# A two-block network on one core: the head norms of attention branch C computed chunk by chunk instead of in one table at the end

## The chip, the cores and the metric

The kernel runs on one core of a Trainium2 chip. The core has five engines that run side by side, each through its own list of instructions in a fixed order: TensorE (PE in the profile; its weight loads are listed apart, as PEld), VectorE (DVE), ScalarE (ACT), GpSimd (POOL), and SyncE (SP), from which all data transfers are started. The metric is the device time of one execution in microseconds (us). Three runs of the kernel before took 1641.73, 1644.12 and 1644.69 us; the median is 1644.12 us.

## The reference

The reference passes 256 tokens of width 1024 through a first block (a mixer of convolution, pooling and attention, then a mixture of experts) and then through two layers of a second block. A layer of the second block is a feed-forward network, a mixer with three attention branches, and another feed-forward network; 16 learned tokens stand in front, so that 272 tokens are processed. The change touches branch C of the mixer, where queries (eight heads of 64) and keys (two heads of 64) are normalised per head before the rotation:

```python
def rms_norm_2(x, g):
    xf = x.astype(jnp.float32)
    y = xf * lax.rsqrt(jnp.mean(xf * xf, axis=-1, keepdims=True) + EPS)
    return (y * g.astype(jnp.float32)).astype(x.dtype)
...
    n = rms_norm_2(h, mix_norm[l])          # the mixer's input
    qa, ka, va, qb, kb, vb, qc, kc, vc, gates = jnp.split(n @ w_in, offsets, axis=-1)
...
    qc = apply_axial_rope(rms_norm_2(heads(qc, C_Q_HEADS), qn), row, col)
    kc = apply_axial_rope(rms_norm_2(heads(kc, C_KV_HEADS), kn), row, col)
    oc = dense_block_attention(qc, kc, heads(vc, C_KV_HEADS))
```

Since every channel of a head is divided by the same number, the division of a query head can be done on its scores later, and that of a key head on the rotated key.

## The kernel before

Everything is stored transposed: 128 channels by 272 tokens in a tile. A linear layer takes its weights from one long stream of units of eight 128x128 tiles, which SP loads into `raw` buffers (line 362). Each chunk of four weight tiles is split in two: ScalarE rounds it to `h` (line 378), and VectorE computes the rest `l = raw - h` (line 395). TensorE then runs three matmuls for each weight tile (lines 509 to 511, `mm3`): `h` with the low part of the input, `h` with its high part, and `l` with its high part. `h` has 9 buffers and `l` 7, and splitting runs some six chunks ahead of the matmuls. So VectorE has to deliver one `l` for each twelve matmuls.

The mixer's input projection (`Mixer.fillers`, section `z0` or `z1` of the stream) has one output tile after the other. For branch C these are, in this order, the key tile `kc`, four query tiles `qc` 0 to 3 (two heads each) and the value tile `vc`. `linear` yields twice in each output tile of eight weight tiles, after four of them each; such a yield is a tick. `Weave.run` counts the ticks: at each it first runs what `after(n, f)` put off until then, and then events of the attention (scores, softmax, transposes), so that the small work of attention stands between the matmuls of the projection. The source order made in this way is then arranged, when the program is built, into one fixed list for each engine: an instruction may be moved past others that it doesn't depend on. On the chip each engine runs its list strictly in order, and waits where an operand isn't ready.

What is done to a `qc` or `kc` tile (`Mixer.evac`): ScalarE copies it out of PSUM and squares it into a tile `t` (line 1553; two such buffers). Two ticks later `head_squares` sums the squares of each head with tiny matmuls into a PSUM tile `ph` (line 1657, three matmuls for 272 tokens), and VectorE copies the sums into a table `ssq` of 3x10 columns (line 1659). After the last one, `qc` 3, `norm_c` turns the whole table into factors: `rsqrt` computes mean plus epsilon on VectorE (`rsa`, line 558), then raises it to the power -0.5 on GpSimd (`rsy`, line 559). Line 1668 multiplies the eight query columns by 1/8 on VectorE; the result `qscale` later scales the scores. Three ticks on, `keys` spreads the key columns over the channels with matmuls into `pb` (line 620, `spread`), multiplies the rotated key by them (line 1672) and cuts the key into parts `kk` and `kl` (lines 1605 to 1607, the last a transfer on SP). In the first layer, `meta` computes `mscale` for the 16 extra tokens five ticks on.

Besides, the value tile `vc` is scaled into `t` on VectorE (line 1544), transposed on TensorE into `pv` (line 1627), and its last 16 tokens are laid out by six GpSimd instructions in `vd` (lines 1642 to 1644), which TensorE transposes into `pw` (line 1632). The first block ends with the convolution's last activation on ScalarE (`cv`, line 1059), a small product `pc`, and its result `mix` (line 1069), which the last output product needs.

Of the kernel before, what the change touches and what calls it, by code (L numbers as in the profile page):

```python
# [7 lines left out]
F32 = mybir.dt.float32  # L8
# [4 lines left out]
ALU = mybir.AluOpType  # L13
# [5 lines left out]
S = 256  # L19
META = 16  # L20
T = S + META
EPS = 1e-6
# [5 lines left out]
HD = 64  # L28
# [421 lines left out]
class Kernel:  # L450
# [97 lines left out]
        o, _ = PARAMS[name]  # L548
        return self.par[:, o + j:o + j + n]

    def rsqrt(self, src, shape, mul, add=EPS):

        v = self.nc.vector
        a, y = (self.tiny.tile(shape, F32, name="rs" + n, bufs=2) for n in "ay")
        if isinstance(add, float):
            v.tensor_scalar(a, src, mul, add, op0=ALU.mult, op1=ALU.add)
        else:
            v.scalar_tensor_tensor(a, src, mul, add, op0=ALU.mult, op1=ALU.add)
        self.nc.gpsimd.tensor_tensor(y, a, self.halves[:, :1].to_broadcast(shape), op=ALU.pow)  # L559
        self.radicand = a  # L560
        return y
# [145 lines left out]
class Block1:  # L707
# [243 lines left out]
    def head_squares(self, kind, i, s):  # L951
        K, nc = self.K, self.nc
        c = 2 * (i % 2) + (kind == "k")
        if c == 0:
            self.ssq = self.p2.tile([128, 2, 8], F32, name="ssq1")
        q = K.ps.tile([128, 512], F32, name="ph", tag="t", bufs=2)
        for j in range(2):
            nc.tensor.matmul(q[:, 2 * j:2 * j + 2], s[:, 128 * j:128 * j + 128], K.table("half"), start=True, stop=True)
        nc.vector.tensor_copy(self.ssq[:, :, 2 * c:2 * c + 2], q[:, :4].rearrange("p (j r) -> p j r", r=2))
        if c == 3:  # L960
            self.norm_qk(i - 1)
# [533 lines left out]
class Mixer:  # L1495
# [7 lines left out]
    def run(self, after):  # L1503
        K, nc, l, n = self.K, self.nc, self.l, self.n
        self.gates = K.big.tile([128, 24, T], F32, name="gates", tag="bigA")
        self.ob = K.big.tile([128, 24, T], F32R, name="ob", tag="bigB")
        self.oh, self.ol = self.ob[:, :12], self.ob[:, 12:]
        self.rb = K.norm_rows(T)
        self.ssq = None
        self.after = K.after  # L1510
        first = 18 if n == T else 16
        K.weave.run(self.fillers(), self.events(), first, 2 * len(Z_MS) + 18)
        self.finish(after)


    def fillers(self):
# [7 lines left out]
    def evac(self, m, p):  # L1524
        K, nc = self.K, self.nc
        kind, i = Z_MS[m]
# [20 lines left out]
        if kind in ("qb", "kb"):  # L1547
            self.parts(kind, i, z)
        elif kind in ("vb", "va", "vc"):
            self.values(kind, i, z)  # L1550
        elif kind in ("qc", "kc"):
            s = K.tmp.tile([128, T], F32, name="t2")[:, :w]
            nc.scalar.activation(s, p, AF.Square)
            self.after(2, lambda: self.head_squares(kind, i, s))

    def swap(self, kind, i, z):

# [86 lines left out]
        nc.gpsimd.tensor_copy(d[:, b], d[:, a])  # L1644

    def head_squares(self, kind, i, s):
        K, nc = self.K, self.nc
        w = s.shape[1]
        if self.ssq is None:
            self.ssq = K.tiny.tile([128, 3, 10], F32, name="ssq")  # L1650
            if self.n == S:
                nc.gpsimd.memset(self.ssq, 0.0)
        c = 4 if kind == "kc" else i
        p = K.ps.tile([128, 512], F32, name="ph", tag="t", bufs=2)
        cuts = [0, 128] if w == S else [0, 128, T - 128]
        for j, o in enumerate(cuts):
            nc.tensor.matmul(p[:, 2 * j:2 * j + 2], s[:, o:o + 128], K.table("half"), start=True, stop=True)  # L1657
        nj = len(cuts)
        nc.vector.tensor_copy(self.ssq[:, :nj, 2 * c:2 * c + 2], p[:, :2 * nj].rearrange("p (j r) -> p j r", r=2))
        if (kind, i) == ("qc", 3):  # L1660
            self.norm_c()

    def norm_c(self):

        K, nc = self.K, self.nc
        y = K.head_rsqrt(self.ssq, [128, 3, 10])
        self.qscale = K.tiny.tile([128, 3, 8], F32, name="qscale", bufs=1)
        nc.vector.tensor_scalar(self.qscale, y[:, :, :8], HD ** -0.5, None, op0=ALU.mult)

        def keys():  # L1670
            z = self.turned_c.pop(("kc", 0))
            nc.vector.tensor_mul(z, z, K.spread(y[:, :, 8:10], T))
            self.parts("kc", 0, z)

        def meta():

            d = K.tmp.tile([128, 8, META], F32, name="vq", bufs=1)
            nc.gpsimd.tensor_tensor(d, K.table("ident")[:, 128 - META:].unsqueeze(1).to_broadcast([128, 8, META]),
                                    self.qscale[:, 2].unsqueeze(2).to_broadcast([128, 8, META]), op=ALU.mult)
            p = K.ps.tile([128, 512], F32, name="pq", tag="t", bufs=2)  # L1680
            nc.tensor.matmul(p[:, :1], d.rearrange("p c m -> p (c m)"), K.table("ones")[:, :1], start=True, stop=True)
            self.mscale = K.tiny.tile([128, 1], F32, name="mscale", bufs=1)
            nc.vector.tensor_copy(self.mscale, p[:, :1])

        self.after(3, keys)
        if self.n == T:
            self.after(5, meta)


    def events(self):  # L1690
# [265 lines left out]
```

## Time and profile before

| | |
|---|---|
| median of three runs | 1644.12 us (1641.73 to 1644.69) |
| the profiled execution | 1641.68 us |
| its span, first to last instruction | 1639.8 us |
| TensorE busy | 1590.8 us, 97% |
| VectorE busy | 1153.9 us, 70% |
| ScalarE busy | 955.9 us, 58% |
| GpSimd busy | 255.9 us, 16% |
| mean granted TensorE clock | 0.987 of full speed |

The profile shows one execution. A row of the timeline gives the start, the duration, the engine, the line, the operation and its tiles; in brackets stands how long the engine had been idle before it, and which instruction ended that. The table of windows gives busy times in a stretch and the granted clock of TensorE, as a share of full speed. [...] The two mixers of the second block, in which the change lies, run their projections from about 515 us (first layer) and 1190 us (second layer).

### The profile page before, as it was taken

What the parts mean: (1) busy time and instruction counts of PE and PEld (TensorE: products, weight loads), DVE (VectorE), ACT (ScalarE), POOL (GpSimd) and SP (SyncE); (2) the same over time, 40 slices, a digit from 0 to 9 for tenths busy, and PEclk for the clock granted to TensorE, in tenths of its full rate; (3) what the DMA queues carried; (4) which work ended last, traced back from release to release, by engine and by line L of the source; (5) the groups of instructions that cost most, each with busy time, mean ns of one, the idle gap of its engine ahead of it and who ended that gap; (6) DMA issues with size and microseconds to landing.
All of it is one profiled execution on the core that took longest, in us unless ns stands there. A gap on an engine that the chain in (4) does not pass through costs nothing.

```text
span 1639.8 us, 32660 instructions
## 1 busy us (share of the span) xinstructions
PE 1590.8 (97%) x12034; PEld 1517.1 (93%) x12034; DVE 1153.9 (70%) x2433; ACT 955.9 (58%) x2002; POOL 255.9 (16%) x493
## 2 busy tenths in 40 slices
PE   7989999899999989999999999999998999999997
PEld 6877777799999979999999999999998999999997
DVE  6757888867666867668777666766677776877753
ACT  7526777655554757665655555555566776565552
POOL 2111000200001444342000010000034333200000
PEclk9999999999999999999999999999999999999998
DMA  7336889355554534454555555555553454455552
GB/s 265 104 134 226 333 309 322 131 179 173 175 175 159 168 113 134 148 166 155 182 171 177 171 177 168 177 171 179 169 170 127 139 166 158 161 193 189 183 189 82
DMA packets 87253, 289.80 MB, mean 177 GB/s; under 512 B 11696, under 2 KB 17328, under 8 KB 86960
## 3 DMA queue, kind: packets, MB, share of 16 engines
q1 hardware_dynamic: 87088, 287.66, 52.3%
q8 instruction: 96, 1.57, 0.4%
q14 instruction: 69, 0.57, 0.1%
HBM read 282.18 MB, written 1.05 MB: 173 GB/s over the span
## 4 chain that ended last, share of the span: by engine, by line
PE 74%; DVE 3%; POOL 2%; issue 1%; ACT 1%; DMA 0%; SPq 0%; DVEq 0%; POOLq 0%; ACTq 0%
PE acc L509 23%; PE acc L511 23%; PE acc L510 23%; PE po L1873 1%; PE pt L1849 1%; DVE l L395 1%; PE sc L1812 1%; PE sc L1813 1%; POOL rsy L559 1%; PE pb L620 0%; DVE ob L1597 0%; DVE xl L579 0%; PE pt L1859 0%; PE ph L1657 0%; DMA zs<-gates 0%
## 5 line engine op out<-in xcount | busy, mean ns | idle before, releaser
L378 ACT ACTIVATE h<-raw 128x512 fp32r<-128x512 f32 x996 | 621.7, 631 | 509.8 <-PE acc L510 400.3
L395 DVE TENSOR_TENSOR l<-raw,h 128x512 fp32r<-128x512 f32 x996 | 692.2, 701 | 232.1 <-PE acc L511 197.8
L509 PE MATMUL acc<-xl,h 128*128 128x272 f32 (+1 forms) x2288 | 669.7, 293 | 6.9 <-ACT h L378 6.8
L511 PE MATMUL acc<-xh,l 128*128 128x272 f32 (+1 forms) x2288 | 659.0, 288 | 0.8 <-DVE l L395 0.8
L510 PE MATMUL acc<-xh,h 128*128 128x272 f32 (+1 forms) x2288 | 656.9, 287 | 0.0
L509 PEld LDWEIGHTS acc<-xl,h 128*128 128x128 f32 x2288 | 434.6, 190 | 16.0 <-issue 8.2
L511 PEld LDWEIGHTS acc<-xh,l 128*128 128x128 f32 x2288 | 434.2, 190 | 1.1 <-DVE l L395 1.0
L510 PEld LDWEIGHTS acc<-xh,h 128*128 128x128 f32 x2288 | 434.5, 190 | 0.2
L511 PE MATMUL acc<-ah,l 128*128 128x272 f32 (+1 forms) x704 | 202.2, 287 | 0.0
L509 PE MATMUL acc<-al,h 128*128 128x272 f32 (+1 forms) x704 | 202.2, 287 | 0.0
L510 PE MATMUL acc<-ah,h 128*128 128x272 f32 (+1 forms) x704 | 201.5, 286 | 0.0
L595 POOL TENSOR_TENSOR sqacc<-sqacc,sq 128x272 f32<-128x272 f32 (+1 forms) x53 | 45.4, 857 | 797.5 <-ACT sq L591 796.6
L511 PEld LDWEIGHTS acc<-ah,l 128*128 128x128 f32 x704 | 132.7, 188 | 0.0
L509 PEld LDWEIGHTS acc<-al,h 128*128 128x128 f32 x704 | 132.6, 188 | 0.0
L510 PEld LDWEIGHTS acc<-ah,h 128*128 128x128 f32 x704 | 132.6, 188 | 0.0
L509 PE MATMUL acc<-ob,h 128*128 128x272 f32 (+1 forms) x320 | 92.5, 290 | 0.0
L510 PE MATMUL acc<-ob,h 128*128 128x272 f32 (+1 forms) x320 | 90.9, 284 | 0.0
L511 PE MATMUL acc<-ob,l 128*128 128x272 f32 (+1 forms) x320 | 90.8, 285 | 0.0
L664 DVE TENSOR_TENSOR t<-acc,rb 128x272 f32<-128x272 f32 (+1 forms) x88 | 38.5, 437 | 63.5 <-PE acc L511 63.5
L1777 POOL TENSOR_SCALAR P<-P,r 128x272 f32<-128x272 f32 x48 | 54.8, 1142 | 122.8 <-DVE r L1775 101.1
L509 PEld LDWEIGHTS acc<-ob,h 128*128 128x128 f32 x320 | 60.2, 188 | 2.0 <-issue 1.2
L510 PEld LDWEIGHTS acc<-ob,h 128*128 128x128 f32 x320 | 60.3, 188 | 0.0
(353 smaller groups left out, 1999.5 us busy)
## 6 DMA issues: line engine op xcount, KB each, us to landing
raw<-in_stream_dram SPq DMA_DIRECT2D x523, 512.0 KB, 3.3
bias<-in_rpb_dram SPq DMA_DIRECT2D x16, 272.0 KB, 3.2
zs<-gates SPq DMA_DIRECT2D x48, 34.0 KB, 2.2
kk<-kk SPq DMA_DIRECT2D x24, 68.0 KB, 2.0
X<-in_x_dram SPq DMA_DIRECT2D x4, 256.0 KB, 5.5
tab<-in_tables_dram SPq DMA_DIRECT2D x1, 1024.0 KB, 7.2
zs<-gates SPq DMA_DIRECT2D x32, 32.0 KB, 2.2
out_dram<-out SPq DMA_DIRECT2D x4, 256.0 KB, 2.2
```

The costliest lines, as they stand in the source:

```text
L378: self.nc.scalar.activation(h, src, AF.Copy)
L395: self.nc.vector.tensor_sub(l, src, h.bitcast(F32))
L509: mm(out, h, xl, start=start, stop=False)
L510: mm(out, h, xh, start=False, stop=False)
L511: mm(out, l, xh, start=False, stop=stop)
L559: self.nc.gpsimd.tensor_tensor(y, a, self.halves[:, :1].to_broadcast(shape), op=ALU.pow)
L595: (nc.vector if k == KC - 1 else nc.gpsimd).tensor_add(self.sqs[0], self.sqs[0], s)
L664: nc.vector.tensor_mul(u, p, rb)
L1777: (nc.gpsimd if h else nc.vector).tensor_scalar(P[:, h, keys], P[:, h, keys], r[:, h:h + 1], None, op0=ALU.mult)
L1812: nc.tensor.matmul(sc[h][:, :T], q[:, h, s], k[:, h], start=True, stop=False)
L1813: nc.tensor.matmul(sc[h][:, :T], q[:, h, s], kl[:, h], start=False, stop=True)
L1849: nc.tensor.transpose(p[:, 128 * (2 * c + h):128 * (2 * c + h) + 128], P[:, h, 128 * c:128 * c + 128], ident)
```

## The change

`norm_c` and the table `ssq` are gone. `head_squares` now runs four ticks after the tile instead of two, and finishes its own columns: VectorE adds the epsilon straight from PSUM, and GpSimd raises six columns (four for the queries of the second layer) to the power. For queries the result goes straight into `qscale`: the factor 1/8 is folded in by working with the sum instead of the mean and with 64 times epsilon (`scaled_eps`, a small GpSimd instruction, one for each layer). For the key, `norm_keys` runs four ticks after its squares, instead of three after `qc` 3. `meta_scale` runs four ticks after `qc` 3's squares.

```diff
--- before.py
+++ after.py
@@ -548,10 +548,12 @@
         o, _ = PARAMS[name]
         return self.par[:, o + j:o + j + n]
 
-    def rsqrt(self, src, shape, mul, add=EPS):
+    def rsqrt(self, src, shape, mul, add=EPS, y=None):
 
         v = self.nc.vector
-        a, y = (self.tiny.tile(shape, F32, name="rs" + n, bufs=2) for n in "ay")
+        a = self.tiny.tile(shape, F32, name="rsa", bufs=2)
+        if y is None:
+            y = self.tiny.tile(shape, F32, name="rsy", bufs=2)
         if isinstance(add, float):
             v.tensor_scalar(a, src, mul, add, op0=ALU.mult, op1=ALU.add)
         else:
@@ -1506,11 +1508,16 @@
         self.ob = K.big.tile([128, 24, T], F32R, name="ob", tag="bigB")
         self.oh, self.ol = self.ob[:, :12], self.ob[:, 12:]
         self.rb = K.norm_rows(T)
-        self.ssq = None
         self.after = K.after
+        self.after(3, self.scaled_eps)
         first = 18 if n == T else 16
         K.weave.run(self.fillers(), self.events(), first, 2 * len(Z_MS) + 18)
         self.finish(after)
+
+    def scaled_eps(self):
+
+        self.eps_head = self.K.tiny.tile([128, 3], F32, name="epsh", bufs=1)
+        self.nc.gpsimd.tensor_scalar(self.eps_head, self.K.eps_tok, float(HD), None, op0=ALU.mult)
 
 
     def fillers(self):
@@ -1551,7 +1558,7 @@
         elif kind in ("qc", "kc"):
             s = K.tmp.tile([128, T], F32, name="t2")[:, :w]
             nc.scalar.activation(s, p, AF.Square)
-            self.after(2, lambda: self.head_squares(kind, i, s))
+            self.after(4, lambda: self.head_squares(kind, i, s))
 
     def swap(self, kind, i, z):
 
@@ -1644,47 +1651,42 @@
         nc.gpsimd.tensor_copy(d[:, b], d[:, a])
 
     def head_squares(self, kind, i, s):
+
         K, nc = self.K, self.nc
         w = s.shape[1]
-        if self.ssq is None:
-            self.ssq = K.tiny.tile([128, 3, 10], F32, name="ssq")
-            if self.n == S:
-                nc.gpsimd.memset(self.ssq, 0.0)
-        c = 4 if kind == "kc" else i
         p = K.ps.tile([128, 512], F32, name="ph", tag="t", bufs=2)
         cuts = [0, 128] if w == S else [0, 128, T - 128]
+        nj = len(cuts)
         for j, o in enumerate(cuts):
             nc.tensor.matmul(p[:, 2 * j:2 * j + 2], s[:, o:o + 128], K.table("half"), start=True, stop=True)
-        nj = len(cuts)
-        nc.vector.tensor_copy(self.ssq[:, :nj, 2 * c:2 * c + 2], p[:, :2 * nj].rearrange("p (j r) -> p j r", r=2))
-        if (kind, i) == ("qc", 3):
-            self.norm_c()
-
-    def norm_c(self):
-
-        K, nc = self.K, self.nc
-        y = K.head_rsqrt(self.ssq, [128, 3, 10])
-        self.qscale = K.tiny.tile([128, 3, 8], F32, name="qscale", bufs=1)
-        nc.vector.tensor_scalar(self.qscale, y[:, :, :8], HD ** -0.5, None, op0=ALU.mult)
-
-        def keys():
-            z = self.turned_c.pop(("kc", 0))
-            nc.vector.tensor_mul(z, z, K.spread(y[:, :, 8:10], T))
-            self.parts("kc", 0, z)
-
-        def meta():
-
-            d = K.tmp.tile([128, 8, META], F32, name="vq", bufs=1)
-            nc.gpsimd.tensor_tensor(d, K.table("ident")[:, 128 - META:].unsqueeze(1).to_broadcast([128, 8, META]),
-                                    self.qscale[:, 2].unsqueeze(2).to_broadcast([128, 8, META]), op=ALU.mult)
-            p = K.ps.tile([128, 512], F32, name="pq", tag="t", bufs=2)
-            nc.tensor.matmul(p[:, :1], d.rearrange("p c m -> p (c m)"), K.table("ones")[:, :1], start=True, stop=True)
-            self.mscale = K.tiny.tile([128, 1], F32, name="mscale", bufs=1)
-            nc.vector.tensor_copy(self.mscale, p[:, :1])
-
-        self.after(3, keys)
-        if self.n == T:
-            self.after(5, meta)
+        ssq = p[:, :2 * nj].rearrange("p (j r) -> p j r", r=2)
+        shape = [128, nj, 2]
+        if kind == "kc":
+            y = K.rsqrt(ssq, shape, 1.0 / HD, K.eps_tok.unsqueeze(2).to_broadcast(shape))
+            self.after(4, lambda: self.norm_keys(y))
+            return
+        if i == 0:
+            self.qscale = K.tiny.tile([128, 3, 8], F32, name="qscale", bufs=1)
+        K.rsqrt(ssq, shape, 1.0, self.eps_head[:, :nj].unsqueeze(2).to_broadcast(shape), self.qscale[:, :nj, 2 * i:2 * i + 2])
+        if i == 3 and self.n == T:
+            self.after(4, self.meta_scale)
+
+    def norm_keys(self, y):
+        K, nc = self.K, self.nc
+        z = self.turned_c.pop(("kc", 0))
+        nc.vector.tensor_mul(z, z, K.spread(y, T))
+        self.parts("kc", 0, z)
+
+    def meta_scale(self):
+
+        K, nc = self.K, self.nc
+        d = K.tmp.tile([128, 8, META], F32, name="vq", bufs=1)
+        nc.gpsimd.tensor_tensor(d, K.table("ident")[:, 128 - META:].unsqueeze(1).to_broadcast([128, 8, META]),
+                                self.qscale[:, 2].unsqueeze(2).to_broadcast([128, 8, META]), op=ALU.mult)
+        p = K.ps.tile([128, 512], F32, name="pq", tag="t", bufs=2)
+        nc.tensor.matmul(p[:, :1], d.rearrange("p c m -> p (c m)"), K.table("ones")[:, :1], start=True, stop=True)
+        self.mscale = K.tiny.tile([128, 1], F32, name="mscale", bufs=1)
+        nc.vector.tensor_copy(self.mscale, p[:, :1])
 
 
     def events(self):
```

How the change moves instructions: three places. The first is VectorE in the first layer, where branch C's last norms fall (`rsa`, `ssq` and `qscale` as above; `t` is the scaled value tile or a gate, `ob` the low parts of queries). Before:

```order
L1659 COPY ssq<-ph 128x3x2
L1842 TENSOR_REDUCE mpm<-pt 96x64
L558 SCALAR_TENSOR_TENSOR rsa<-ssq,eps_7975 128x30
L395 TENSOR_TENSOR l<-raw,h 128x512
L1597 TENSOR_TENSOR ob<-gates,ob 64x272 x2
L1668 TENSOR_SCALAR qscale<-rsy 128x24
L1544 TENSOR_TENSOR t_8861<-acc,rb 128x272
L395 TENSOR_TENSOR l<-raw,h 128x512
L1576 SCALAR_TENSOR_TENSOR gates<-gates,par,tab 128x272
L1577 SCALAR_TENSOR_TENSOR zs<-zs,par,tab 128x272
```

and now, from the reduction `mpm` on:

```order
L1844 TENSOR_REDUCE mpm<-pt 96x64
L395 TENSOR_TENSOR l<-raw,h 128x512
L1604 TENSOR_TENSOR ob<-gates,ob 64x272 x2
L1551 TENSOR_TENSOR t_8879<-acc,rb 128x272
L395 TENSOR_TENSOR l<-raw,h 128x512
L1583 SCALAR_TENSOR_TENSOR gates<-gates,par,tab 128x272
L1584 SCALAR_TENSOR_TENSOR zs<-zs,par,tab 128x272
L560 SCALAR_TENSOR_TENSOR rsa<-ph,epsh 128x6
L1585 TENSOR_TENSOR gates<-gates,zs 128x272
```

The multiplication that reads the power's result is gone from the list, and the scaled value tile follows the two subtractions `ob` directly; one `rsa` of six columns stands behind the rotation of `qc` 3.

The second place is GpSimd in the same stretch (`P` is the second head's softmax, `Pm`, `PTm` and `qd` small copies of attention, `vd` the value tile's extra tokens). Before:

```order
L1777 TENSOR_SCALAR P<-P,r 128x272
L1642 CAST Pm<-P 128x32
L1643 TENSOR_TENSOR Pm<-P,Pm 128x32
L1644 COPY Pm<-Pm 128x32
L1863 CAST PTm<-mpm 96x16
L559 TENSOR_TENSOR rsy<-rsa,halves 128x30
L1863 CAST PTm<-mpm 96x16
L1796 COPY qd<-ob 128x16 x2
L1678 TENSOR_TENSOR vq<-core,qscale 128x128
L1642 CAST vd<-t_8861 64x16 x2
L1643 TENSOR_TENSOR vd<-t_8861,vd 64x16
L1644 COPY vd<-vd 64x16
```

and now:

```order
L1779 TENSOR_SCALAR P<-P,r 128x272
L561 TENSOR_TENSOR qscale<-rsa,halves 128x3x2
L1649 CAST Pm<-P 128x32
L1650 TENSOR_TENSOR Pm<-P,Pm 128x32
L1651 COPY Pm<-Pm 128x32
L1865 CAST PTm<-mpm 96x16 x2
L1798 COPY qd<-ob 128x16 x2
L1649 CAST vd<-t_8879 64x16 x2
L1650 TENSOR_TENSOR vd<-t_8879,vd 64x16
L1651 COPY vd<-vd 64x16
L1650 TENSOR_TENSOR vd<-t_8879,vd 64x16
L1651 COPY vd<-vd 64x16
```

The power of 30 columns has become powers of 3x2 columns; the one of `qc` 2 now stands right behind `P` and ahead of `Pm`, and the one of `qc` 1 stands ahead of the `qd` copies before this piece; the last comes after the six `vd` instructions.

The third place is ScalarE at the end of the first block, which the diff doesn't touch (`cv` is the convolution's activation, two tiles). Before:

```order
L1059 ACT_TABLE_LOAD
L1059 ACTIVATE cv_135<-cv_135,par 128x256
L1059 ACTIVATE cv_136<-cv_136,par 128x256
L378 ACTIVATE h<-raw 128x512 x2
L1069 ACTIVATE mix<-pc,par 128x256
L378 ACTIVATE h<-raw 128x512
L1069 ACTIVATE mix<-pc,par 128x256
L378 ACTIVATE h<-raw 128x512 x6
```

and now:

```order
L1061 ACTIVATE cv_135<-cv_135,par 128x256
L378 ACTIVATE h<-raw 128x512 x2
L1061 ACTIVATE cv_136<-cv_136,par 128x256
L378 ACTIVATE h<-raw 128x512 x2
L1071 ACTIVATE mix<-pc,par 128x256 x2
L378 ACTIVATE h<-raw 128x512 x5
L589 ACTIVATE sqacc<-X 128x256
L593 ACTIVATE sq_1442<-X 128x256
```

Two weight splits now stand between the two tiles of the convolution. On TensorE, in both layers, the sums `ph` of each tile have moved behind 12 further matmuls of the projection and the score matmuls among them; `pb` has moved from behind `pv` to where `qc` 1's `ph` now stands; and in the first layer `pw` comes four projection matmuls after `pv`, where it came after `pb` and one. On SP, the two transfers of the key now stand four `raw` loads earlier or less.

## Rows read from the trace of the kernel before

**Rows 1.** Page: busy time of an engine, its share of the span, instructions.

```profile
PE 1590.8 (97%) x12034; PEld 1517.1 (93%) x12034; DVE 1153.9 (70%) x2433; ACT 955.9 (58%) x2002; POOL 255.9 (16%) x493
```

**Rows 2.** Timeline, first layer: start, duration, engine, line, operation, [idle before, releaser].

```profile
575.87 5.13 POOL L559 TENSOR_TENSOR rsy<-rsa,halves 128x30 f32<-128x30 f32 x1
581.03 0.18 DVE L1668 TENSOR_SCALAR qscale<-rsy 128x24 f32<-128x24 f32 x1 [5.33 <-POOL rsy L559]
581.12 0.43 DVE L1544 TENSOR_TENSOR t<-acc,rb 128x272 f32<-128x272 f32 x1
581.61 0.69 PE L1627 MATMUL pv<-core,t 128*128 128x128 f32 x2 [5.37 <-DVE t L1544]
```

**Rows 3.** Timeline, second layer: the same chain.

```profile
1248.83 0.18 DVE L1668 TENSOR_SCALAR qscale<-rsy 128x24 f32<-128x24 f32 x1 [4.83 <-POOL rsy L559]
1251.23 0.69 PE L1627 MATMUL pv<-core,t 128*128 128x128 f32 x2 [4.92 <-DVE t L1544]
```

**Rows 4.** Timeline: the sums of the key's squares, both layers.

```profile
550.87 0.83 PE L1657 MATMUL ph<-core,t 128*128 128x2 f32 x6 [1.80 <-ACT t L1553]
1224.17 0.83 PE L1657 MATMUL ph<-core,t 128*128 128x2 f32 x6 [1.23 <-ACT t L1553]
```

**Rows 5.** Windows: length, busy PE, PEld, DVE, ACT, POOL, granted clock, DMA share, GB/s.

```profile
545.00:587.00 42.00, 34.74 (x252) 33.30 (x250) 31.82 (x99) 27.17 (x73) 22.89 (x45) 0.88 0.40 127
1210.00:1256.30 46.30, 38.94 (x298) 37.42 (x296) 37.23 (x106) 30.37 (x77) 20.10 (x30) 0.89 0.45 147
550.00:560.00 10.00, 9.13 (x62) 9.13 (x63) 8.06 (x27) 7.09 (x21) 4.87 (x10) 0.83 0.61 184
1225.00:1230.00 5.00, 5.00 (x31) 5.00 (x31) 3.07 (x10) 3.48 (x11) 1.55 (x4) 0.66 0.61 189
581.60:587.00 5.40, 5.35 (x28) 4.57 (x28) 4.63 (x13) 2.71 (x9) 2.80 (x9) 0.52 0.18 46
1251.20:1256.30 5.10, 5.07 (x32) 4.82 (x32) 4.64 (x13) 2.72 (x7) 3.38 (x10) 0.54 0.30 105
587.00:625.00 38.00, 38.00 (x302) 35.92 (x302) 28.14 (x79) 26.66 (x68) 13.94 (x33) 1.00 0.44 140
```

**Rows 6.** Groups by line: count, busy time, mean ns; idle before, releaser.

```profile
L559 POOL TENSOR_TENSOR rsy<-rsa,halves 128x30 f32<-128x30 f32 x2 | 10.3, 5129 | 2.2 <-DVE rsa L558 2.2
L559 POOL TENSOR_TENSOR rsy<-rsa,halves 128x3 f32<-128x3 f32 x5 | 4.4, 878 | 35.2 <-DVE rsa L556 35.2
```

**Rows 7.** Timeline, GpSimd in the projections (the last two rows: second layer).

```profile
560.51 0.21 POOL L1642 CAST vd<-vq 128x32 fp32r<-128x32 f32 x1 [4.69 <-DVE vq L1836]
567.06 0.67 POOL L1796 CAST qd<-ob 128x16 fp32r<-128x16 f32 x2 [5.85 <-DVE ob L1597]
581.72 1.08 POOL L1642 CAST vd<-t 64x16 fp32r<-64x16 f32 x2
583.59 0.41 POOL L1644 CAST vd<-vd 64x16 fp32r<-64x16 f32 x1
1251.24 0.44 POOL L1642 CAST vd<-t 64x16 fp32r<-64x16 f32 x2 [2.44 <-DVE d L1771]
1252.56 0.20 POOL L1644 CAST vd<-vd 64x16 fp32r<-64x16 f32 x1
```

**Rows 8.** By line: VectorE's copies of the sums, shortest, mean, longest.

```profile
L1659 DVE COPY ssq<-ph x10: 151/156/168, 552.3 to 1241.7; 128x6 f32<-128x6 f32 x6, 128x4 f32<-128x4 f32 x4
```

**Rows 9.** Timeline, first block: a power of 16 columns beside weight splits.

```profile
29.39 2.92 POOL L559 TENSOR_TENSOR rsy<-rsa,halves 128x16 f32<-128x16 f32 x1 [6.53 <-DVE rsa L558]
29.64 1.29 DVE L395 TENSOR_TENSOR l<-raw,h 128x512 fp32r<-128x512 f32 x2 [0.34 <-issue]
```

**Rows 10.** Timeline, ScalarE where the first block ends.

```profile
118.98 0.91 ACT L1059 ACTIVATE cv<-cv,par 128x256 f32<-128x256 f32 x2 [4.61 <-DVE cv L1058]
121.21 1.15 ACT L378 ACTIVATE h<-raw 128x512 fp32r<-128x512 f32 x2 [1.32 <-DMA raw<-in_stream_dram]
```

## The prediction

> **What bounds the kernel now.** I read the page's busy times first: TensorE is busy 1590.8 us, 97% of the span, and VectorE 1153.9 us [rows 1]. So TensorE sets the time, and a change off TensorE pays only where it takes away a wait of TensorE, or time that TensorE spends at its lower clock. The timeline then shows the waits around the change. In the first layer the power of 30 columns runs on GpSimd from 575.87 us for 5.13 us; VectorE idles 5.33 us for it in front of `qscale`, the value tile's `t` is queued behind that, and TensorE idles 5.37 us in front of `pv` [rows 2]. The second layer repeats it: 4.83 and 4.92 us [rows 3]. A second, smaller wait stands at the key: `ph` needs ScalarE's square, and TensorE idles 1.80 us for it in the first layer and 1.23 us in the second [rows 4]. The table of windows shows what each wait leaves behind: the granted clock is 0.83 in the ten microseconds around the key's wait, 0.66 and 0.52 to 0.54 behind the others, and 1.00 in 587 to 625 us, where TensorE doesn't pause [rows 5]. [...] So a wait costs its own length and, behind it, the missing share of the clock times the stretch.
>
> **The change part by part.** All is worked out on the profiled execution, 1641.68 us, with a span of 1639.8 us. The three timed runs lie 0.05 to 3.0 us above it, their median 2.4.
>
> *The power's wait goes.* VectorE has no instruction behind a power any more; `t` follows the two `ob` directly, so `pv` can start when TensorE reaches it. First layer: 5.37 us, and 5.40 us at a granted clock of 0.52, that is 5.40 x 0.48 = 2.59; together 7.96 [rows 2, 5]. Second layer: 4.92, and 5.10 x 0.46 = 2.35; together 7.27 [rows 3, 5]. Sum 15.2 us.
>
> *The key's wait goes.* With four ticks instead of two, 12 more matmuls stand ahead of `ph`. At 38.00 us for 302 instructions, 0.126 us each [rows 5], that is 1.5 us, and the score matmuls add to it; the longer of the two waits is 1.80. First layer: 1.80 + 10.00 x 0.17 = 3.50; second layer: 1.23 + 5.00 x 0.34 = 2.93 [rows 4, 5]. Sum 6.4 us. Bounds: if the score matmuls took no time, 0.3 us of the first wait would stay. For the query tiles the same two ticks only add slack.
>
> All four together are 21.7 us. Three things give some of it back.
>
> *GpSimd in the first layer.* A power takes 5.129 us for 30 columns and 0.878 for 3 [rows 6]: 4.251 / 27 = 0.157 us for a column and 0.41 for the start. So six columns take 1.35 us and four 1.04. The first layer has five of 1.35, 6.8 us in place of 5.13; the second one of 1.35 and four of 1.04, 5.5 us. The powers of the key and of `qc` 0 fall where GpSimd idled, 4.69 and 5.85 us [rows 7]. Those of `qc` 1 and `qc` 2 stand ahead of `qd` and of the six `vd` instructions, for which TensorE's `pw` waits. GpSimd had finished the work ahead of the power at 575.87; with 0.2 for `PTm`, 0.4 for `qd`, two powers of 1.35 and the `vd` chain's 2.28 (581.72 to 584.00) it is done at 581.3 at the latest [rows 2, 7]. `pw` would be due at about 578: `pv` at 576.24 (581.61 less its wait of 5.37), its own 0.7 and some matmuls. So `pw` waits between 0 (if GpSimd's idle times hide both powers) and 3.3 us. I take 2.2, since one of the two may be partly hidden, and 1.7 behind it for the clock, as behind the wait of 1.80: 3.9, bounds 0 and 5.7. In the second layer the `vd` chain takes 1.5 us (1251.24 to 1252.76), and `pw` stands only at the end of the 5.1 us behind `pv`, which at a granted clock of 0.54 is 2.8 us of work at the higher level, 2.2 without `pb` [rows 5, 7]. One power of 1.04 in the way would make 0.3 us of waiting; I take nothing, since GpSimd idled there (2.44 us).
>
> *VectorE becomes tight.* Without these losses TensorE would need 42.00 - 11.46 = 30.5 us in the first stretch and 46.30 - 10.2 = 36.1 in the second. VectorE is busy 31.82 and 37.23 us there [rows 5]. Its own share changes little: five copies of 0.156 [rows 8], `rsa` and a `qscale` of 0.18 go, 1.1 us for a layer, and five `rsa` straight from PSUM come, by the copies' and `qscale`'s rows about 0.17 each. So VectorE is fuller than TensorE by about 1 us in each layer, and must borrow from the `l` that lie ready at the start. If the stock covers it, it costs nothing; if not, 2.4 us in all and the clock behind it, up to 5. I take 2.5.
>
> *The end of the first block.* The scheduler has put two weight splits between the two `cv` on ScalarE. Two splits take 1.15 us and two `cv` 0.91, and ScalarE idled 1.32 us for a transfer behind them [rows 10]. So the second `cv` and what hangs on it can come up to 1.2 us later, or the splits fill that idle time. I take 0.4, bounds -0.5 and 1.5.
>
> Edits at nothing: `scaled_eps` runs while GpSimd idles; without that cover it costs a few tenths once for each layer. The key's transfers are moved past at most four `raw` loads on SP, with `h` and `l` several chunks ahead; uncovered, a late load stops TensorE by one transfer at most. The squares' buffers are held two ticks longer: two buffers serve tiles that come two ticks apart, so ScalarE's next-but-one square comes after the `ph` that frees its buffer; uncovered, it waits as `ph` does now. The new `rsa` reads PSUM, as the copy did, so the slot is freed after the same kind of instruction.
>
> Sum: 21.7 - 3.9 - 2.5 - 0.4 = 14.9, so 1626.8 us on the profiled execution's scale. A median lies a little above that; I add 0.7 and say 1627.5.
>
> **The rivals.** (A) Nothing is given back: `pw` finds `vd` done and the stock of `l` covers VectorE. For it speaks that GpSimd idles 10.5 us in the stretch before [rows 7]; against it, that VectorE is fuller than TensorE. 1641.7 - 21.7 + 0.7 = 1620.7.
>
> (B) VectorE is the bound in both stretches and keeps the rest of its idle time, 42.00 - 31.82 - 5.33 = 4.85 us and 46.30 - 37.23 - 4.83 = 4.24 [rows 2, 3, 5]. Then only its waits for the power, 10.2 us, are gained: 1631.5 + 0.7 = 1632.2. For it speaks VectorE's load; against it, that part of this idle time was waiting for TensorE's slow stretches, which go too.
>
> (C) The wait only moves: TensorE stands before `pb` for the key's power, or before `pw` for a whole queue of powers, some 5 us in each layer. Then only the key's 6.4 us are left, 1636. Against it: `pb` has four ticks, two output tiles' work, for a power of 1.35.
>
> (D) A power stops VectorE's subtractions while it runs. In the rows, a power of 16 columns ran from 29.39 to 32.31, and two subtractions from 29.64 took 1.29 us, 0.65 each, with 0.34 idle ahead for issue [rows 9]: not stopped. If they were stopped, VectorE, which is the tight one, would lose the powers' 6.8 + 5.5 = 12.3 us: 1627.5 + 12.3 = 1639.8, within 0.2% of the profiled execution. [...]
>
> (E) Slower: in place of four long waits come many short ones of TensorE on a full VectorE, spread over the whole stretch, so that the clock never rises. [...] Against it: from 587 us on VectorE is 74% busy (28.14 of 38.00) and the clock is 1.00 [rows 5].
>
> **How the numbers follow.** The forecast has 0.50, with its own range 1623 to 1631 from the bounds of the three terms. A has 0.15, B 0.20, C 0.03, D 0.07, E 0.05. The range of 8 in 10 takes in A and B with a little behind each: 1620 to 1634; C, D, E and the outer edge of A are left out. A measurement here can tell 0.2%, 3.3 us, from no change. The forecast, A, B and C are faster by more than that, 0.88; D is the same, 0.07; E is slower, 0.05.
>
> **What would show it.** In the profile of the changed kernel: `pv` in both layers without a wait for VectorE, and the clock behind it near 1.00; the key's `ph` with less than 0.4 us of waiting; powers of 1.3 to 1.4 us for six columns; a wait of 1 to 3 us at `pw` in the first layer, released by GpSimd's `vd`; short waits of TensorE for `l` in the stretches, 2 to 3 us in sum; about 6 us less between the same instructions around the first layer's stretch, and 9 around the second's. I am wrong if TensorE waits for a power anywhere by over 2 us, if subtractions beside powers take longer than their 0.7, or if the stretches' clock stays under 0.95 without a single long wait.

## The result, and the profile after

The changed kernel took 1624.03 us (median of 4 runs, 1623.42 to 1625.68); the kernel before, timed beside it, 1644.4 us (4 runs, 1641.73 to 1646.97). The ratio is 0.988, with a 95% interval of 0.9867 to 0.9893. Forecast were 1627.5, from 1620 to 1634. The profiled execution of the changed kernel took 1623.47 us, 18.2 less than that of before.

The page's busy times, as in [rows 1]:

```profile
PE 1584.6 (98%) x12034; PEld 1510.2 (93%) x12034; DVE 1153.1 (71%) x2429; ACT 954.7 (59%) x2002; POOL 258.1 (16%) x502
```

The timeline of TensorE at the places of [rows 2 to 4]: the key's `ph` and the value tile's `pv` and `pw`, first layer, then second.

```profile
552.24 0.72 PE L1661 MATMUL ph<-core,t 128*128 128x2 f32 x6
573.79 0.38 PE L1634 MATMUL pv<-core,t 128*128 128x128 f32 x2
576.53 0.31 PE L1639 MATMUL pw<-core,vd 128*96 128x128 f32 x1 [1.86 <-POOL vd L1651]
1216.01 0.73 PE L1661 MATMUL ph<-core,t 128*128 128x2 f32 x6
1236.12 0.38 PE L1634 MATMUL pv<-core,t 128*128 128x128 f32 x2
1238.13 0.27 PE L1639 MATMUL pw<-core,vd 128*96 128x128 f32 x1
```

No bracket stands at `ph` and `pv`: the four waits of 1.80, 1.23, 5.37 and 4.92 us are gone. One new wait of 1.86 us stands at `pw`, released by GpSimd. GpSimd's rows around it, as in [rows 7]:

```profile
566.74 1.35 POOL L561 TENSOR_TENSOR qscale<-rsa,halves 128x6 f32<-128x6 f32 x1
571.64 1.34 POOL L561 TENSOR_TENSOR qscale<-rsa,halves 128x6 f32<-128x6 f32 x1
575.18 0.44 POOL L1649 CAST vd<-t 64x16 fp32r<-64x16 f32 x2
576.28 0.20 POOL L1651 CAST vd<-vd 64x16 fp32r<-64x16 f32 x1
576.56 1.32 POOL L561 TENSOR_TENSOR qscale<-rsa,halves 128x6 f32<-128x6 f32 x1
```

A power of six columns takes 1.35 us, and those of `qc` 1 and 2 (566.74, 571.64) stand ahead of `vd`, which ends 0.05 us before `pw` starts. How much of the 1.86 us is theirs, the experiments show. The windows, with the columns of [rows 5]: the two stretches, and the 8 us behind the wait.

```profile
536.00:579.00 43.00, 41.13 (x329) 39.25 (x327) 39.50 (x113) 31.80 (x82) 29.13 (x55) 0.98 0.51 164
1200.00:1243.00 43.00, 41.29 (x347) 39.93 (x346) 41.68 (x120) 35.17 (x94) 21.56 (x35) 1.00 0.55 173
576.80:584.80 8.00, 8.00 (x52) 6.64 (x51) 4.49 (x12) 5.53 (x15) 3.38 (x6) 0.79 0.20 70
```

The clock is 0.98 and 1.00 where it had been 0.88 and 0.89; VectorE is busy 39.50 and 41.68 of 43 us.

To see where the time went, I set the starts of the same weight-stream matmuls (line 509, 3312 in each trace) side by side, and took the difference to before at five of them, which start at 545, 596, 613, 1221 and 1268 us in the trace of before. What a kernel gains from 545 to 596 us is the first layer's share, from 613 to 1221 that of the weight streams between, from 1221 to 1268 the second layer's:

| kernel | timed, us | first layer | 613 to 1221 us | second layer | `h` starts at |
|---|---|---|---|---|---|
| before | 1642 to 1644 | 0 | 0 | 0 | 64n |
| changed | 1624.0 | -7.6 | -1.8 | -9.4 | 64n + 32 |
| ticks alone | 1631.7 | -7.9 | +0.2 | -4.5 | 64n |
| chunks, two ticks | 1630.0 | -3.7 | -1.8 | -7.2 | 64n + 32 |
| multiply back | 1631.6 | -4.1 | -1.8 | -8.4 | 64n + 32 |
| power of 18 | 1623.9 | -10.0 | +0.3 | -9.6 | 64n |
| before, 32 bytes | 1639.8 | -1.8 | -2.1 | -1.6 | 64n + 32 |
| changed, 32 bytes | 1626.3 | -7.7 | +0.3 | -9.9 | 64n |
| power of 18, 32 bytes | 1622.0 | -10.0 | -1.5 | -9.8 | 64n + 32 |
| ticks, keys late | 1626.9 | -8.3 | +0.1 | -6.9 | 64n |
| vector load | 1628.9 | -5.0 | -2.2 | -8.6 | 64n + 32 |
| pw late | 1621.8 | -11.2 | -2.0 | -9.1 | 64n + 32 |
| all three | 1620.9 | -11.2 | -1.6 | -9.5 | 64n + 32 |
| changed, again | 1624.4 | -7.6 | -1.7 | -9.6 | 64n + 32 |

The last column is the byte address of the first `h` buffer in the built program. The rest of each difference lies ahead of 545 us, where nearly the same lists differ by up to 4.5 us from execution to execution, and behind 1268. The shares of the changed kernel came out again within 0.2 us. Those of the kernel before hold some luck: with 32 bytes it has the same waits in both layers and is 1.8 and 1.6 us shorter there, because the clock behind the key's waits stayed at 1.00 in that execution.

### The profile page after: what moved, and what is told of

The parts are those of the page before. It is cut to its first block, busy times and chain, and to the rows that moved or that the text cites. A ratio compares the mean times of both kernels' runs of the same rounds, so it can differ in the third digit from the quotient of the medians.

```text
span 1621.2 us, 32667 instructions
## 1 busy us (share of the span) xinstructions
PE 1584.6 (98%) x12034; PEld 1510.2 (93%) x12034; DVE 1153.1 (71%) x2429; ACT 954.7 (59%) x2002; POOL 258.1 (16%) x502
## 4 chain that ended last, share of the span: by engine, by line
PE 75%; DVE 3%; issue 1%; POOL 1%; DMA 0%; SPq 0%; ACT 0%; DVEq 0%; POOLq 0%; ACTq 0%
PE acc L509 23%; PE acc L511 23%; PE acc L510 23%; PE po L1875 2%; PE pt L1851 1%; DVE l L395 1%; PE sc L1814 1%; PE sc L1815 1%; DVE ob L1604 0%; PE pt L1861 0%; PE pb L622 0%; DVE P L1754 0%; DVE xl L581 0%; PE pn L606 0%; SPq L1568 0%
## 5 line engine op out<-in xcount | busy, mean ns | idle before, releaser
L509 PEld LDWEIGHTS acc<-xl,h 128*128 128x128 f32 x2288 | 432.0, 189 | 16.2 <-issue 8.6
```

What stands on the lines that cost most here:

```text
L509: mm(out, h, xl, start=start, stop=False)
```

## The experiments

The kernel before was timed again beside the experiments, on four chips: its medians were 1642.5 to 1643.6, its runs 1637.6 to 1647.3 us. A ratio is that to before, with its 95% interval.

**Ticks alone.** The kernel before, with one edit:

```diff
-            self.after(2, lambda: self.head_squares(kind, i, s))
+            self.after(4, lambda: self.head_squares(kind, i, s))
```

> The kernel before with one number changed: the sums of squares run four ticks after the tile instead of two. The table of 30 columns, the single power of 5.13 us and VectorE's qscale behind it stay. Theory A (the prediction's sum taken literally, the change's two parts add up): the key's two waits go, the power's stay: 6.4 us less than before, about 1638. Theory B (it is the place in VectorE's list that counts): with four ticks the value tile's t stands ahead of qscale, so no work of TensorE is directly behind the power; VectorE still idles some 4 to 5 us for it, TensorE goes on from the 4 to 5 chunks of l that lie ready (1.5 us each), and the vd chain now stands ahead of the power, so TensorE's pw doesn't wait either: 1621 to 1626, as good as the whole change or better.

1631.67 us, 0.9933 (0.9916 to 0.9949): neither 1638 nor 1624. TensorE in the first layer and in the second:

```profile
571.52 0.38 PE L1627 MATMUL pv<-core,t 128*128 128x128 f32 x2
573.93 0.31 PE L1632 MATMUL pw<-core,vd 128*96 128x128 f32 x1 [1.28 <-POOL vd L1644]
579.42 0.73 PE L620 MATMUL pb<-core,rsy 128*64 128x128 f32 x12 [0.77 <-POOL rsy L559]
1245.45 1.25 PE L620 MATMUL pb<-core,rsy 128*64 128x128 f32 x12 [3.97 <-POOL rsy L559]
```

VectorE in the second:

```profile
1245.43 0.18 DVE L1668 TENSOR_SCALAR qscale<-rsy 128x24 f32<-128x24 f32 x1 [4.91 <-POOL rsy L559]
```

`pv` waits for nothing, though VectorE still stands 4.91 us behind the power: `t` is ahead of it now. TensorE waits for the power itself, in front of the key's `pb`. So half of theory B holds, and most of the rest of the time lies where neither theory put it. By the table this one number gains as much in the first layer as the whole change (7.9 us for 7.6); the second layer, with the wait of 3.97 us, makes the difference.

Theory B was wrong on `pw`: it waits 1.28 us although the power stands behind `vd`. GpSimd's instructions for `vd` alone run from 571.28 to 573.88, and the power begins behind them:

```profile
571.28 1.13 POOL L1642 CAST vd<-t 64x16 fp32r<-64x16 f32 x2
573.68 0.20 POOL L1644 CAST vd<-vd 64x16 fp32r<-64x16 f32 x1
574.23 5.13 POOL L559 TENSOR_TENSOR rsy<-rsa,halves 128x30 f32<-128x30 f32 x1
```

**Chunks at two ticks.** The changed kernel with `after(2, ...)` instead of `after(4, ...)`.

> The changed kernel with two ticks instead of four. Theory A: the power's waits are gone (no VectorE operation behind a power), the key's two waits of TensorE for ScalarE's square are back, 1.8 and 1.2 us and the slower clock behind them, 6.4 us in all; the powers come two ticks earlier, so that fewer stand ahead of the vd chain and pw's 1.86 us are smaller or gone (0 to -3.5): 1627 to 1631. Theory B (the two ticks do nearly everything, the chunked powers little): well over 1631, towards 1638.

1630.0 us, 0.9922 (0.9904 to 0.994): theory A's range, by other parts than it said.

```profile
550.61 0.83 PE L1661 MATMUL ph<-core,t 128*128 128x2 f32 x6 [1.80 <-ACT t L1560]
579.52 0.31 PE L1639 MATMUL pw<-core,vd 128*96 128x128 f32 x1 [3.68 <-POOL vd L1651]
1218.12 0.83 PE L1661 MATMUL ph<-core,t 128*128 128x2 f32 x6 [1.15 <-ACT t L1560]
```

The key's waits are back as expected. But `pw` waits 3.68 us instead of less: two ticks earlier, the power of `qc` 3 and `vq` also stand ahead of `vd` on GpSimd.

**The multiplication back**, behind each query power:

```diff
-        K.rsqrt(ssq, shape, 1.0, self.eps_head[...]..., self.qscale[:, :nj, 2 * i:2 * i + 2])
+        y = K.rsqrt(ssq, shape, 1.0 / HD, K.eps_tok[...]...)
+        nc.vector.tensor_scalar(self.qscale[:, :nj, 2 * i:2 * i + 2], y, HD ** -0.5, None, op0=ALU.mult)
```

> The changed kernel with VectorE's multiplication by 1/8 back behind each of the four query powers, in chunks of 6 columns (epsilon and mean as before). If an operation of VectorE behind a power costs TensorE its wait (the prediction's step), four waits of 1.4 to 3 us appear on VectorE, which is 96 to 98% busy in these stretches, and TensorE loses part of them: 4 to 10 us in both layers, 1628 to 1634. If the l that lie ready cover short waits, at most 2 us: 1624 to 1626.

1631.56 us, 0.9928 (0.9913 to 0.9943). VectorE waits four times in the first layer:

```profile
562.92 0.16 DVE L1671 TENSOR_SCALAR qscale<-rsy 128x6 f32<-128x6 f32 x1 [1.79 <-POOL rsy L561]
572.22 0.17 DVE L1671 TENSOR_SCALAR qscale<-rsy 128x6 f32<-128x6 f32 x1 [1.61 <-POOL rsy L561]
579.06 0.16 DVE L1671 TENSOR_SCALAR qscale<-rsy 128x6 f32<-128x6 f32 x1 [2.02 <-POOL rsy L561]
584.86 0.16 DVE L1671 TENSOR_SCALAR qscale<-rsy 128x6 f32<-128x6 f32 x1 [1.66 <-POOL rsy L561]
```

and TensorE waits for `t`, which stands behind the third again:

```profile
581.41 0.41 PE L1634 MATMUL pv<-core,t 128*128 128x128 f32 x2 [1.67 <-DVE t L1551]
```

By the table this costs 3.5 us in the first layer and 1.0 in the second. The wait at `pv` is only part of the 3.5: TensorE also stands 0.91 us before a score and 0.92 us before a transpose there, and 1.16 instead of 1.86 at `pw`. Of the 5.9 us by which the profiled span is longer, 1.8 lie ahead of 310 us, which these edits don't reach: behind a wait of 2.27 us that both executions have, the clock was 0.70 here and 1.00 in the changed kernel.

**A power of 18 columns** for queries 1 to 3, behind `vd`:

```diff
+        nc.vector.scalar_tensor_tensor(self.rad[:, :nj, 2 * i - 2:2 * i], ssq, 1.0, ..., op0=ALU.mult, op1=ALU.add)
+        if i == 3:
+            nc.gpsimd.tensor_tensor(self.qscale[:, :nj, 2:], self.rad[:, :nj], K.halves[...], op=ALU.pow)
```

> The changed kernel with one power of 18 columns for queries 1 to 3 in place of three of 6 columns. The two powers of 1.35 us ahead of the vd chain in the first layer are gone; the one power (0.41 + 18 x 0.157 = 3.2 us) stands behind that chain. If the wait of 1.86 us at pw and the lower clock of 0.79 in the 8 us behind it are GpSimd's powers in the way, both go: 3.5 us less than the changed kernel, 1620.5. If something else holds the vd chain (its t, VectorE), pw keeps its wait: 1624.

1623.86 us, 0.9881 (0.9862 to 0.9899): the stretch gained, the total didn't.

```profile
577.30 0.31 PE L1639 MATMUL pw<-core,vd 128*96 128x128 f32 x1 [1.18 <-POOL vd L1651]
```

```profile
577.40:586.00 8.60, 8.60 (x69) 7.88 (x70) 6.84 (x22) 6.25 (x17) 6.34 (x10) 1.00 0.40 127
```

The wait fell from 1.86 to 1.18 and left no slower clock behind it (1.00 instead of 0.79): 2.4 us less in the first layer. So the expectation is half right: 1.18 us of the wait stay with no power between `P` and `vd` on GpSimd, as 1.28 us did with ticks alone. So the two powers cost 0.7 us of waiting and 1.7 of clock; the rest goes to GpSimd's other instructions, those for `vd` among them. And from 613 to 1221 us, where the lists are those of the changed kernel, 2.1 us were lost.

**32 bytes.** An unused tile moves everything behind the small tiles. The edit is the same for the kernel before, the changed one and that with the power of 18:

```diff
         self.eps_tok = self.tiny.tile([128, w], F32, name=f"eps{w}", bufs=2)
+        if w == 3:
+            self.tiny.tile([128, 8], F32, name="pad", bufs=1)
```

> The kernel before, with one unused tile of 32 bytes in the pool of small tiles: every tile that is laid out behind that pool (h, l, raw and others) starts 32 bytes later, the lists stay as they are. In the traces the same matmuls of the weight stream start 126.1 ns apart in some stretches (320 to 450 us, 860 to 1100 us) in the kernel before, with ticks alone and with the power of 18, and 125.3 in the changed kernel, with two ticks and with the multiply back; h starts at a multiple of 64 bytes in the first three and 32 past one in the others. If the place of the tiles does that, this kernel shows 125.3 ns there and is 1.5 to 3 us faster than before, about 1641.5 where before has 1643.5. If it is chance or the instruction order, nothing moves: 1643.5 and 126.1 ns.

> The changed kernel with the same unused 32 bytes; h now starts at a multiple of 64. Theory place: 126.1 ns in those stretches, 1.5 to 3 us slower than the changed kernel, about 1626. Theory chance: 125.3 ns or a mix, 1624.

> The kernel with one power of 18 columns for queries 1 to 3, with the same unused 32 bytes; h now starts 32 past a multiple of 64. Its trace without them had gained 2.3 us around the first layer's pw against the changed kernel and lost about as much by the slower matmuls elsewhere. Theory place: 125.3 ns, about 2 us faster than without, 1621.5, and so faster than the changed kernel. Theory chance: 1624.

Before with 32 bytes: 1639.77 us, 0.9987 (0.9974 to 1.0). The changed kernel with them: 1626.32, 0.9899 (0.9882 to 0.9917). The power of 18 with them: 1622.03, 0.9873 (0.9855 to 0.9891). How many matmuls fit into the same 100 us, by windows on TensorE alone (length, busy PE with count, granted clock, DMA share, GB/s), in the kernel before, in it with 32 bytes, in the changed kernel, and in that with 32 bytes:

```profile
340.00:440.00 100.00, 100.00 (x795) 1.00 0.52 174
```

```profile
340.00:440.00 100.00, 100.00 (x801) 1.00 0.54 178
```

```profile
340.00:440.00 100.00, 100.00 (x801) 1.00 0.55 176
```

```profile
340.00:440.00 100.00, 100.00 (x795) 1.00 0.53 175
```

795 or 801, at the same clock of 1.00, by the place of the tiles and not by the kernel; with the power of 18 it is 796 without the 32 bytes and 800 with them. From 320 to 450 us the mean spacing of neighbouring matmuls of the weight stream (steps under 200 ns) is 126.1 or 125.3 ns, from 860 to 1100 us 126.1 or 125.5. Some stretches show no difference, and from 1460 to 1510 us it is the other way about, 118.3 or 118.9. Chance doesn't explain it: all fourteen traces fall in the group of their addresses. The times alone wouldn't show it, as the runs of each pair overlap and the ratio of before with 32 bytes reaches 1.0; but all three moved as the place says, by 1.8 to 2.7 us. So the changed kernel owes some 2 us to where its other tiles came to lie, and the part that its instructions earned is, at equal place, 1642.48 - 1626.32 = 16.2 us or 1639.77 - 1624.03 = 15.7.

**Ticks and late keys.** The kernel before with `after(4, ...)` for the squares and, behind the table's power:

```diff
-        self.after(3, keys)
+        self.after(6, keys)
```

> The kernel before with four ticks for the sums of squares and six instead of three for the keys behind the power. One table, one power of 30 columns, and VectorE's qscale behind it stay. With ticks alone TensorE waited for the power itself in front of pb, 0.77 us in the first layer and 3.97 in the second, while VectorE's 3.6 and 4.9 us of idling for it cost TensorE nothing. If that is right, both waits of pb go and the time falls from 1631.7 by 4.7 and some clock to 1624 to 1626.5, as good as the whole change without taking VectorE's operation away. If VectorE's idling counts after all, TensorE waits elsewhere for l or P and the time stays at 1630 to 1632.

1626.92 us, 0.99 (0.9882 to 0.9918). Both waits for the power at `pb` are gone; in the first layer `pb` now waits 1.11 us for VectorE's `mscale`. VectorE's idling now costs TensorE something in the second layer, in front of a score that waits for VectorE's maximum `m`:

```profile
1247.23 0.39 PE L1812 MATMUL sc<-kk,ob 128*128 128x272 f32 x1 [1.52 <-DVE m L1752]
```

At the same place of the tiles the change takes 1626.32; by the table the two stretches are 2.4 us behind it (15.2 for 17.6). So two numbers in the old kernel give all but 0.6 to 2.4 us of what the change gives, with the one power of 30 columns and VectorE's operation behind it left in. The expectation's 1624 to 1626.5 was missed by 0.4.

**Vector load.** Two multiplications more for each branch C tile:

```diff
+        x = K.tiny.tile([128, T], F32, name="xtra", bufs=1)[:, :w]
+        for _ in range(2):
+            nc.vector.tensor_mul(x, s, s)
```

> The changed kernel with two extra VectorE multiplications (the squares' tile by itself, 128x272, into a scratch tile that nobody reads) for each of the five branch C tiles: some 0.43 us each, 4.3 us more VectorE work in each layer. The prediction took VectorE for fuller than TensorE by 1 us in each layer and charged 2.5 us. If that is right, 4.3 us more in each layer cost close to their own length: 1630 to 1634. If the chunks of l that lie ready (3 to 6 in the changed kernel, 1.5 us each) cover it, 1624 to 1626.

1628.88 us, 0.9918 (0.9899 to 0.9937), between the two. Two groups of lines (VectorE's extra work, and the matmuls that read `l`):

```profile
L1659 DVE TENSOR_TENSOR xtra<-t 128x272 f32<-128x272 f32 (+1 forms) x20 | 8.7, 434 | 0.0
L511 PE MATMUL acc<-xh,l 128*128 128x272 f32 (+1 forms) x2288 | 655.3, 286 | 0.0
```

8.7 us more work, and no wait for `l` at all. The 3.4 us that the table shows for both layers have one wait in them that isn't VectorE's:

```profile
575.80 1.35 POOL L561 TENSOR_TENSOR qscale<-rsa,halves 128x6 f32<-128x6 f32 x1
577.38 0.20 POOL L1649 CAST vd<-vq 128x32 fp32r<-128x32 f32 x1
578.13 0.31 PE L1845 MATMUL pt<-core,vd 128*96 128x128 f32 x1 [2.05 <-POOL vd L1651]
```

In the lists with the extra instructions, GpSimd's work for this transpose of attention stands behind a power; in the changed kernel it ran at 558.47, long before it was needed. Another 2.1 us of the 5.0 by which the profiled span is longer lie ahead of 545 us. How much of the 4.9 us of time is VectorE's load as such stays open.

**pw late**, in the changed kernel and in the power of 18 with 32 bytes:

```diff
-        self.after(3, meta)
+        self.after(6 if kind == "vc" else 3, meta)
```

> The changed kernel with the value tile's pw six ticks after its tile instead of three (33 more instructions of TensorE ahead of it), nothing else. If the 1.86 us of waiting at pw and the 0.79 of the clock in the 8 us behind it are what GpSimd's powers cost, both go: 3.5 us, to about 1620.5. If another operand is late right behind it (vm for the product po, P), the wait only moves: 1623 to 1624.

> The kernel with one power of 18 columns and the unused 32 bytes, with pw six ticks after its tile instead of three. Its wait at pw was about 1.2 us, without a slower clock behind it: 1.2 us less than without this, about 1620.8. If the late pw delays something, no gain.

The changed kernel with it: 1621.82 us (1621.08 to 1623.86), 0.9876 (0.9855 to 0.9897). The first layer, where before there was a wait and a clock of 0.79:

```profile
574.00:586.00 12.00, 12.00 (x98) 11.27 (x98) 11.18 (x33) 8.08 (x22) 10.03 (x25) 1.00 0.41 135
```

The table shows 3.6 us gained there, as 3.5 were expected; ahead of 545 us this execution happened to be 2.5 later. All three together: 1620.91 (1619.55 to 1623.96), 0.9866 (0.9846 to 0.9887), the fastest median of this study, but not clearly apart from 1621.82.

**The changed kernel again.**

> The changed kernel once more, unchanged, as a measure for the small differences between the experiments. If its median of 1624.0 holds on another day, 1623.5 to 1625.0, the late pw (1621.8) and the power of 18 with 32 bytes and the late pw (1620.9) are really faster. If it comes out at 1622 or less, these differences are those between two calls, and stay open. Its trace tells as well whether the waits at pw (1.86 us) and the 125.3 ns between matmuls are the kernel's or that execution's.

1624.38 us (1623.52 to 1626.95), 0.989 (0.9871 to 0.9909). Its `pw` waits 1.87 us, and its matmuls stand 125.3 ns apart. So by the medians a late `pw` is 2.2 to 2.6 us faster, with little overlap of the runs; the intervals of the ratios overlap, since before itself varies by up to 9 us.

## Why the prediction was right, and where it wasn't

*The power's wait (15.2 us)* and *the key's wait (6.4)*: right. All four waits are gone. But the clock that the prediction counted behind the key's wait, 1.70 us in each layer, comes and goes. With 32 bytes the kernel before has the same wait of 1.81 us and a clock of 1.00 in the ten us around it:

```profile
551.00:561.00 10.00, 8.20 (x66) 8.20 (x67) 9.51 (x31) 8.15 (x24) 6.29 (x12) 1.00 0.66 212
```

In the second layer its wait of 1.22 us was followed by 1.00 as well, while that of 1.15 us with chunks at two ticks was followed by 0.72 over six us, and the 1.23 in the kernel before by 0.66 over five. That the trace of before had the low clock in both layers, and so agrees with these two terms, is luck: measured from the trace with 32 bytes, the two stretches of the changed kernel gained 3.4 us less.

*GpSimd in the first layer (3.9)*: right in size and place. 1.86 us of wait for 2.2, and 8.00 x 0.21 = 1.68 of clock for 1.7. The late `pw` shows it: without the wait 3.6 us come back. The six columns took the 1.35 that were worked out. But the powers, to which the prediction put the wait, account for 2.4 of it; the power of 18 and ticks alone still wait 1.18 and 1.28 us. The term's own sum ends at 581.45, not 581.3, and its upper bound of 5.7 isn't worked out from rows: 3.3 and 1.7 make 5.0.

*VectorE becomes tight (2.5)*: the step that failed. VectorE is nearly as full as was said, 92 and 97% of the two windows, where TensorE is busy 96% in each. But the sentence "If the stock covers it, it costs nothing" decides. TensorE waits for `l` 0.3 us in the whole execution (0.8 before), and with 8.7 us more of VectorE's work not at all:

```profile
L511 PE MATMUL acc<-xh,l 128*128 128x272 f32 (+1 forms) x2288 | 655.1, 286 | 0.3 <-DVE l L395 0.3
```

In the two stretches of the table it never waits for `l`; its idle time there is the 1.86 us at `pw` and 0.32 before a transpose behind VectorE's `gates`. So this term is 0.3 at most.

*The end of the first block (0.4)*: no cost to be seen. TensorE's waits for `cv` and `mix` there are 1.77 us in sum instead of 2.43; at 545 us the changed kernel is 0.3 us ahead, far less than executions differ by.

*Not in the sum*: the tiles' place, 1.8 us from 613 to 1221. The diff takes 736 bytes out of the pool of small tiles, and no row of before could tell that a matmul would mind.

So the two stretches gave 7.6 + 9.4 = 17.0 us. The sum had 21.7 - 3.9 - 2.5 = 15.3 for them; with the failed term at 0 it would have been 17.8, and the remaining 0.8 is within what the clock term can do. The total of 18.2 us between the profiled executions needs the 1.8 us of the place besides, which no term had. So the 3.5 us between the forecast of 1627.5 and the 1624.0 are in the main 2.2 to 2.5 charged too much for VectorE and 1.8 of place, less the 0.8. The forecast's own range of 1623 to 1631 is also narrower than the bounds of its terms make it, about 1620 to 1633. Rival A's price is what the late `pw` reached (1621.8 for 1620.7), with 2.0 us of the place in it. B fell with the wait for `l`. C didn't come here, but its mechanism is real: with ticks alone TensorE waited 3.97 us for the power at `pb`. E fell with a clock of 0.98 and 1.00.

D, that a power stops VectorE, is refuted by the rows. VectorE's `l` and `ob` beside two powers:

```profile
559.82 0.69 DVE L395 TENSOR_TENSOR l<-raw,h 128x512 fp32r<-128x512 f32 x1
571.76 0.90 DVE L1604 TENSOR_TENSOR ob<-gates,ob 64x272 fp32r<-64x272 f32 x2
```

and the power that began at 559.93:

```profile
559.93 1.77 POOL L561 TENSOR_TENSOR qscale<-rsa,halves 128x6 f32<-128x6 f32 x1
```

`ob` began 0.12 us after the power at 571.64, which ran to 572.98, and the two took 0.90 us, 0.45 each, where the median `ob` of this kernel takes 0.435. The other power took 1.77 us instead of 1.35 beside an `l` that began before it. So the longer row is GpSimd's, not VectorE's. Over all fourteen traces, the 142 subtractions `l` that began while a power ran took 0.689 us on average and none over 0.694; the others took 0.700.

The reason given for the gain holds in one part only. What paid is that the value tile's `t` no longer stands behind a power, that the key's `pb` doesn't come to wait for one instead, and that the squares' sums come later; ticks and late keys do that too. VectorE's operation as such is worth what the multiplication back cost: 3.5 us in the first layer, where `t` stood behind it, and 1.0 in the second, where `pv` didn't wait.

## What to carry to other kernels

An engine's idle time behind a slow operation cost TensorE here through what was queued behind it: with ticks alone VectorE stood 4.91 us behind the power in the second layer, with `t` ahead of it, and `pv` waited for nothing. So look in the order for the next instruction that the bounding engine needs, and move that, before taking the slow operation apart. When operations are split into chunks, look on the engine that runs them for what each chunk now stands in front of; here two small powers made up 2.4 us of what `pw` cost, and a later `pw` gave back all 3.6. And compare a change that adds or drops a tile with a kernel in which the other tiles keep their place, or the share of the address, 1.8 to 2.7 us here, is taken for its merit.

## What the runs showed of the hardware

From 320 to 450 us the same matmuls at the same clock of 1.00 stood 125.3 or 126.1 ns apart, 0.6%, depending on whether the buffers behind the small tiles began 32 bytes past a multiple of 64 or on one; from 1460 to 1510 us it was 118.9 against 118.3. Which of the moved buffers does it, and why, was not tried.

The clock behind a pause of TensorE of 1 to 2.3 us wasn't settled by its length in these traces: over ten us it was 0.83 around a pause of 1.80 and 1.00 around one of 1.81, over five us it was 0.70 or 1.00 behind 2.27. Yet at one place it repeated: behind `pw`'s 1.83 to 1.87 us it was 0.66 over five us in all three traces that have that pause, and the pauses of 4.9 us and more in front of `pv` were followed by 0.52 to 0.60, over 5.1 to 6.0 us, each time. A term that rests on one short pause of one execution belongs in the range, not in the sum.

VectorE's subtraction `l = raw - h` wasn't held by a GpSimd power that was running: 0.689 us on average for the 142 that began during one, against 0.700 otherwise.
